# Down projection: tiles 15 to 18 as a second block group of seven products

## The chip, the cores and the metric

The kernel runs on one core of a Trainium2 chip. The metric is the device time of one execution in microseconds (us). TensorE (PE) multiplies; VectorE (DVE) and ScalarE (ACT) move results out of PSUM, the accumulators of PE, and prepare operands; GpSimd (POOL) and SyncE (SP) mostly issue DMA transfers here. Each engine works through its own queue in order, and waits at an instruction whose inputs or buffers aren't ready.

## The reference

A two-layer encoder over 1040 positions (16 learned ones and 1024 of the input) with 1024 channels. Each layer adds two things to the residual h: attention with its output projection, and a gated feed-forward network. The change lies in the last product of the second:

```
def conv_ffn(x, w_up, conv_w, conv_b, w_down):
    h = x @ w_up
    ...
    u, g = jnp.split(hc, 2, axis=-1)
    return (jax.nn.silu(g) * u) @ w_down

h = h + conv_ffn(rms_norm(h, ffn_norm[i]), w_up[i], conv_w[i], conv_b[i], w_down[i])
```

`w_down` has 2816 rows: 22 tiles of 128 channels. Everything is float32.

## The kernel before

**Numbers.** Channels lie on the 128 partitions, positions along the free axis. Each float32 operand of PE is split into a rounded part and the rest ("hi" and "lo", or ah and al), and a product is three matmuls: hi by hi, lo by hi, hi by lo (`mm3`, lines 254 to 256). Weights are loaded raw by SP, ACT casts the hi part, and DVE subtracts to get the lo part (lines 1132 and 1133 in `up_split`, 221 and 223 in `weights`).

**The down projection** sums 22 inner tiles for eight output tiles m of 128 channels and two halves of the positions (520 and 520 in layer 0, in pieces of 260 columns; 512 and 512 in layer 1, where the 16 learned positions are no longer wanted). It takes the inner tiles in five groups, listed in `GROUPS, LAST` (line 49):

- tiles 0 to 2, kind "n": for each m and half, all inner tiles are multiplied into one PSUM sum. ACT copies it to a buffer "do" (line 1677; three buffers in turn), and POOL adds that buffer to the residual tile `hm[m]` in DRAM with an accumulating DMA (line 1679).
- tiles 3 to 10, kind "s", a block group: two output tiles, the two halves of the positions and the two halves of the inner tiles make a 2 by 2 block product, done by Strassen's scheme (in Winograd's form) with seven products in place of eight. `down_blocks` has four pairs of output tiles, so 28 products, in an order written out by hand (`seq`). Each product needs a stationary operand made of the four raw weight blocks of its pair (A11, A12, A21, A22 and sums of them; `block_operand`, line 1114 for the sums), which is prepared `AHEAD` = 4 products ahead (`ensure`), and a moving operand X[p] made of the activations (`prepare`). The results are collected in two buffers of a pair, "du" and "dg" (ACT copies on line 1583, DVE adds on line 1582), and POOL adds them to `hm` in DRAM (lines 1600 and 1604). A buffer goes back to the pool of buffers `LANDING` = 4 products after its DMA was issued.
- tiles 11 to 14 and 15 to 18, kind "r": first SP loads the eight residual tiles from DRAM (`load_residual`, line 1650) into hT; then it goes as for "n", but DVE adds each PSUM sum to hT (line 1675).
- tiles 19 to 21 (`LAST`, in `down_last`): the same into hT, in three pieces of the positions; on the way the norm of what follows is fed (line 1754 the add to h, then the split for the next layer and the sum of squares, POOL's share of that on line 343), and hT is stored or, in layer 1, normalised and written out.

**What sets the order.** PE's order is that of the program text. For the other engines a scheduler orders instructions by its own estimate of when each is ready; it may put an instruction ahead of others that the text has before it. The activations were stored to DRAM by the up projection; `prepare` loads them ("st", line 1458), splits them for the plain groups (lines 1495 and 1496) or builds the fourteen buffers X[p] of a block group (lines 368, 369 and 1517). It is a generator that is advanced a step at a time by `pump`, called after each output tile of a plain group and at some products of a block group, where enough buffers are free. All these tiles share 33 buffers of one size, and six more (`ids`) that last through the feed-forward part of a layer; they are given out first in, first out. Raw weights have a ring of four buffers (tag "raw") and one of seven ("raw2"), operands two rings of three.

**Names that the change touches:** `GROUPS`, `LANDING`, `ensure` and `evacuate` and `run` in `down_blocks`, `load_residual`, `plain` and `run` in `ffn_down`.

Of the kernel before, what the change touches and what calls it, by code (L numbers as in the profile page):

```python
# [10 lines left out]
F32 = mybir.dt.float32  # L11
# [12 lines left out]
T = META + SEQ  # L24
KD = D // 128
# [20 lines left out]

GROUPS, LAST = (("n", 0, 3), ("s", 3, 8), ("r", 11, 4), ("r", 15, 4)), (19, 3)
HALVES, HALVES_LAST, HALVES_OUT = (0, 520, 520), (0, 520, 520), (16, 528, 512)  # L50
AHEAD = 4
LANDING = 4
FETCH = 60
SUB = 20
NSPLIT = 4
# [112 lines left out]
class Kern:  # L168
# [1383 lines left out]
            self.need = next(self.prep)  # L1552
            n -= 1

    def down_blocks(self, lyr, g0, ng, X, pp, fw, halves, after):
# [22 lines left out]
        going = []  # L1578

        def evacuate(i, j, p):  # L1580
            q = st[j]
            add = lambda out, ps: nc.vector.tensor_tensor(out=two(out), in0=ps[:, :pieces, :n], in1=two(out), op=ALU.add)
            copy = lambda out: nc.scalar.copy(two(out), q["a"][:, :pieces, :n])
            if p == 1:
                q["u"] = s.get(F32, "du")
                copy(q["u"][:, t0])
            elif p == 2:
                add(q["u"][:, t0], q["y"])
            elif p == 6:
                copy(q["u"][:, t1])  # L1590
            elif p == 7:
                q["g"] = s.get(F32, "dg")
                copy(q["g"][:, t1])
                if "x" in q:
                    add(q["g"][:, t1], q["x"])
            elif p == 5 and "g" in q:
                add(q["g"][:, t1], q["x"])
            elif p == 4:
                copy(q["g"][:, t0])
                nc.gpsimd.dma_start(self.hm[2 * j + 1][:, o0:T], q["g"][:, o0:T], accum_op=ALU.add)  # L1600
                going.append((i + LANDING, q["g"]))
            elif p == 3:
                add(q["u"][:, t1], q["x"])
                nc.gpsimd.dma_start(self.hm[2 * j][:, o0:T], q["u"][:, o0:T], accum_op=ALU.add)
                going.append((i + LANDING, q["u"]))
                del st[j]
        def run():
            self.among_blocks = True
            for i, (j, p) in enumerate(seq):
                ensure(i + AHEAD)  # L1610
                q = st.setdefault(j, {})
                bank, begins = {2: "y", 5: "x", 3: "x"}.get(p, "a"), p in (1, 2, 5)
                if begins:
                    place = {1: j % 2, 2: 3, 5: 2}[p]
                    q[bank] = pp.tile([128, 2, 512], F32, tag=f"p{place}", name="down", bufs=1)
                ps, w = q[bank], ops[i]
                ops[i] = None
                for k in range(nk):
                    _, hi, lo = X[p][k // 2]
                    for c in range(pieces):  # L1620
                        self.mm3(ps[:, c, :n], w[k], (hi[:, k % 2, :], lo[:, k % 2, :]), c * n, n,
                                 begins and k == 0, k == nk - 1, not begins)
                evacuate(i, j, p)
                while going and (going[0][0] <= i or i == len(seq) - 1):
                    s.put(going.pop(0)[1])
                if j == NP - 1:
                    for held, _, _ in X.pop(p):
                        s.put(*held)
                    if len(ops) == len(seq):
                        after()  # L1630
                    self.pump(1, 3)
                elif j and p == 5:
                    self.pump(1, 4)
            self.among_blocks = False
        return ensure, run

    def ffn_down(self, lyr, pp, fw, halves, acts, X, ids):
# [6 lines left out]
        two = lambda ap: ap.rearrange("p (a b) -> p a b", b=n)  # L1644
        hT, ahead, going = [], [], []

        def load_residual():
            for k in range(KD):
                hT.append(s.get(F32, f"h{k}", first=ids))
                nc.sync.dma_start(hT[k][:, o0:T], self.hm[k][:, o0:T])  # L1650

        def complete(done):
            while not done():
# [5 lines left out]
        def plain(kind, g0, ng, m, w, nxt):  # L1659
            if m == 0:  # L1660
                complete(lambda: all(j in acts for j in range(g0, g0 + ng)))
                if kind == "r" and not hT:
                    load_residual()
            if kind == "n" and m == 0:

                going.extend(s.get(F32, "do") for _ in range(3))
# [37 lines left out]
        def run():  # L1704
            blocks = None
            for i, part in enumerate(parts):
# [202 lines left out]
```

## Time and profile before

| | us |
|---|---|
| median of three runs | 2499.61 (2499.27 to 2500.78) |
| the profiled execution: its time | 2497.96 |
| the profiled execution: its span | 2496.2 |
| layer 0: tiles 11 to 14 and 15 to 18 on PE | 1122.1 to 1214.5 |
| layer 1: the same | 2357.9 to 2446.8 |

The time of an execution holds 1.8 us beside the span from the first to the last instruction. In the rows of stretches below, each engine has its busy time and, in brackets, its number of instructions; PEld is the weight load of PE, which runs beside the matmuls; PEclk is the granted clock of PE as a share of the full one; then come the mean busy share of the 16 DMA engines and what they moved. A row of a group has busy time and the mean of one in ns, and behind the second bar the idle time ahead of it with what ended it. In a row of waits stand the total, the number of times and the longest.

### The profile page before, as it was taken

The page shows a single profiled execution, that of the slowest core. Times are in us where ns is not written, and L with a number is a line of the kernel's source. Part 1 is how long each engine was busy: PE and PEld are TensorE (multiplying, and loading weights), DVE is VectorE, ACT ScalarE, POOL GpSimd, SP SyncE. Part 2 cuts the span into 40 slices and gives each one's busy share as a digit, 9 for nine tenths or more (in the row PEclk, how much of TensorE's full clock was granted, in tenths as well). Part 3 has the DMA queues.
Part 4 walks back from the last instruction along what each step waited for, and adds up shares of the span by engine and source line. Part 5 has one row for each costly group of instructions (what it writes and reads, how often), then busy time and mean ns, then how long its engine had stood idle before and what let it go on. Part 6 is the DMA issues. An engine that isn't in the chain of part 4 may idle for free.

```text
span 2496.2 us, 47323 instructions
## 1 busy us (share of the span) xinstructions
PE 2464.8 (99%) x18358; PEld 2370.8 (95%) x18358; DVE 1837.8 (74%) x3739; ACT 1298.1 (52%) x2811; POOL 385.4 (15%) x567
## 2 busy tenths in 40 slices
PE   9999999999999999999999999999999999999998
PEld 8989999999999999999999899999999999997886
DVE  8656776869988888854666666777699888887536
ACT  7346666636555555641343566665465555555412
POOL 2023333210000000100210334331100000001002
PEclk9999999999999999999999999999999999999999
DMA  3232134343322214763312222243423212247722
GB/s 134 68 88 72 43 97 129 124 126 103 112 84 73 90 65 148 194 172 118 106 56 73 75 78 73 67 147 105 147 88 104 90 66 94 92 151 179 197 72 81
DMA packets 118545, 261.02 MB, mean 105 GB/s; under 512 B 14880, under 2 KB 32544, under 8 KB 118320
## 3 DMA queue, kind: packets, MB, share of 16 engines
q1 hardware_dynamic: 93984, 182.81, 23.3%
q0 software_dynamic: 22464, 72.88, 10.4%
q8 instruction: 144, 2.36, 0.4%
q10 hardware_dynamic: 1872, 2.31, 0.3%
q14 instruction: 81, 0.66, 0.1%
HBM read 177.31 MB, written 67.85 MB: 98 GB/s over the span
## 4 chain that ended last, share of the span: by engine, by line
PE 67%; issue 16%; DVE 11%; ACT 5%; DMA 1%; POOL 0%; SPq 0%; DVEq 0%; POOLq 0%; ACTq 0%
PE mm L254 7%; PE mm L256 7%; PE mm L255 7%; PE up L254 5%; PE up L255 5%; PE up L256 5%; PE down L254 5%; PE down L255 5%; PE down L256 5%; PE av L752 3%; PE tr L726 2%; DVE S L693 1%; PE wo L254 1%; ACT P L705 1%; PE S L690 1%
## 5 line engine op out<-in xcount | busy, mean ns | idle before, releaser
L255 PE MATMUL up<-x,lo 128*128 128x260 f32 x2240 | 633.0, 283 | 0.0
L256 PE MATMUL up<-x,hi 128*128 128x260 f32 x2240 | 632.3, 282 | 0.3 <-DVE x L1157 0.3
L254 PE MATMUL up<-x,hi 128*128 128x260 f32 x2240 | 632.5, 282 | 0.0
L256 PEld LDWEIGHTS up<-x,hi 128*128 128x128 f32 x2240 | 422.2, 188 | 0.6 <-DVE x L1157 0.5
L254 PEld LDWEIGHTS up<-x,hi 128*128 128x128 f32 x2240 | 421.5, 188 | 0.4 <-DVE hg L1370 0.3
L255 PEld LDWEIGHTS up<-x,lo 128*128 128x128 f32 x2240 | 421.3, 188 | 0.1
L254 PE MATMUL mm<-xh,hi 128*128 128x348 f32 (+4 forms) x1056 | 362.6, 343 | 0.0
L256 PE MATMUL mm<-xl,hi 128*128 128x348 f32 (+4 forms) x1056 | 340.1, 322 | 0.0
L255 PE MATMUL mm<-xh,lo 128*128 128x348 f32 (+4 forms) x1056 | 339.5, 321 | 0.0
L1132 ACT CAST hi<-raw 128x512 fp32r<-128x512 f32 (+1 forms) x434 | 243.3, 572 | 150.7 <-PE up L256 88.2
L1133 DVE TENSOR_TENSOR lo<-raw,hi 128x512 fp32r<-128x512 f32 (+1 forms) x434 | 265.0, 624 | 76.0 <-ACT hi L1132 75.6
L254 PEld LDWEIGHTS mm<-xh,hi 128*128 128x128 f32 x1056 | 199.5, 189 | 5.2 <-issue 4.6
L255 PEld LDWEIGHTS mm<-xh,lo 128*128 128x128 f32 x1056 | 199.5, 189 | 0.7 <-issue 0.7
L256 PEld LDWEIGHTS mm<-xl,hi 128*128 128x128 f32 x1056 | 198.4, 188 | 0.4 <-issue 0.3
L221 ACT CAST hi<-raw 128x512 fp32r<-128x512 f32 (+2 forms) x168 | 97.3, 580 | 186.1 <-PE down L256 100.4
L254 PE MATMUL down<-ah,hi 128*128 128x260 f32 (+1 forms) x528 | 168.7, 320 | 0.5 <-ACT do L1677 0.5
L255 PE MATMUL down<-ah,lo 128*128 128x260 f32 (+1 forms) x528 | 168.5, 319 | 0.0
L256 PE MATMUL down<-al,hi 128*128 128x260 f32 (+1 forms) x528 | 168.3, 319 | 0.0
L705 ACT ACTIVATE P<-S,m 116x460 f32<-116x460 f32 (+2 forms) x224 | 124.8, 561 | 71.2 <-DVE m L693 67.5
L369 DVE TENSOR_TENSOR PT<-tr,PT 116x464 fp32r<-116x464 f32 (+3 forms) x240 | 122.9, 515 | 47.5 <-ACT PT L368 45.9
L1114 DVE TENSOR_TENSOR raw<-raw,raw 128x512 f32<-128x512 f32 x198 | 134.6, 686 | 24.1 <-DMA raw<-in_wd_dram 21.9
L1395 POOL DMA_DIRECT2D actd<-cv x44 | 23.6, 535 | 744.0 <-DVE cv L1394 725.9
(308 smaller groups left out, 5962.0 us busy)
## 6 DMA issues: line engine op xcount, KB each, us to landing
raw<-in_wm_dram SPq DMA_DIRECT2D x330, 256.0 KB, 2.9
raw<-in_wd_dram SPq DMA_DIRECT2D x64, 256.0 KB, 3.4
actd<-cv POOLq DMA_DIRECT2D x22, 520.0 KB, 3.0
actd<-cv POOLq DMA_DIRECT2D x22, 512.0 KB, 3.0
cb<-cd SPq DMA_DIRECT2D x16, 520.0 KB, 3.9
hm<-h POOLq DMA_DIRECT2D x32, 260.0 KB, 2.9
st<-actd SPq DMA_DIRECT2D x14, 520.0 KB, 4.4
st<-actd SPq DMA_DIRECT2D x14, 512.0 KB, 4.4
```

The source lines that it names most:

```text
L221: nc.scalar.copy(hi[:, :n, :], raw[:, :n, :])
L254: nc.tensor.matmul(ps, wh, xh[:, c0:c0 + n], start=first, stop=False, skip_group_check=more)
L255: nc.tensor.matmul(ps, wl, xh[:, c0:c0 + n], start=False, stop=False, skip_group_check=more)
L256: nc.tensor.matmul(ps, wh, xl[:, c0:c0 + n], start=False, stop=last, skip_group_check=more)
L369: nc.vector.tensor_tensor(out=lo, in0=src, in1=hi.bitcast(F32), op=ALU.subtract)
L690: nc.tensor.matmul(S[:rows, :n], q["qA"][e][:, qs], q["kA"][e][:, c0:k1], start=True, stop=False)
L705: nc.scalar.activation(P[:rows, :n], S[:rows, :n], AF.Exp, scale=-1.0, bias=m[:rows, nch - 1:nch], accum_out=(den if nch == 1 else d3[:row ...
L726: nc.tensor.transpose(tr[:w, 3 - j, :rows], P[:rows, o:o + w], id_)
L752: nc.tensor.matmul(av[:, a:b], w.rearrange("p a b -> p (a b)"), x, start=(t == ts[0] and part == 0 and i == 0), stop=(t == last and i == 1))
L1114: nc.vector.tensor_tensor(out=q[out][:, :nk, :], in0=q[a][:, :nk, :], in1=q[b][:, :nk, :], op=op)
L1132: nc.scalar.copy(hi[:, :nk, :], src[:, :nk, :])
L1133: nc.vector.tensor_tensor(out=lo[:, :nk, :], in0=src[:, :nk, :], in1=hi[:, :nk, :].bitcast(F32), op=ALU.subtract)
```

## The change

Tiles 11 to 14 become kind "n": ACT copies the sums to the three "do" buffers and POOL adds them to `hm` in DRAM. Tiles 15 to 18 become a second block group of 28 products with two inner tiles per side (nk = 2), half as long as those of the first. The residual stays in DRAM until that group: the tiles of a pair are loaded into hT by SP when both its buffers are given back (`summed`, the pairs 0 and 1), and the rest by POOL at the end of the group. In the second group a buffer is held for eight products instead of four, and the raw weights of the next pair are asked for at product 6 of a pair.

```diff
-GROUPS, LAST = (("n", 0, 3), ("s", 3, 8), ("r", 11, 4), ("r", 15, 4)), (19, 3)
+GROUPS, LAST = (("n", 0, 3), ("s", 3, 8), ("n", 11, 4), ("s", 15, 4)), (19, 3)
...
-LANDING = 4
+LANDING = {4: 4, 2: 8}
...
                 ops.append(self.block_operand(wd(2 * j), wd(2 * j + 1), nk, j, p, fw, raws, len(ops) % 2))
+                if nk == 2 and p == 6 and j + 1 < NP:
+                    self.block_raws(wd(2 * j + 2), wd(2 * j + 3), nk, j + 1, fw, raws)
...
-                going.append((i + LANDING, q["g"]))
+                going.append((i + landing, q["g"], 2 * j + 1))
...
                 while going and (going[0][0] <= i or i == len(seq) - 1):
-                    s.put(going.pop(0)[1])
+                    _, held, m = going.pop(0)
+                    s.put(held)
+                    landed.append(m)
+                    if len(landed) % 2 == 0 and i < len(seq) - 1:
+                        summed(landed[-2:])
...
-        def load_residual():
-            for k in range(KD):
-                hT.append(s.get(F32, f"h{k}", first=ids))
-                nc.sync.dma_start(hT[k][:, o0:T], self.hm[k][:, o0:T])
+        def load_residual(which, engine):
+            for k in sorted(which):
+                assert k == len(hT)
+                hT.append(s.get(F32, f"h{k}"))
+                engine.dma_start(hT[k][:, o0:T], self.hm[k][:, o0:T])
...
-                if kind == "r" and not hT:
-                    load_residual()
...
-                                              lambda t=then: len(ahead) < 2 and fetch(t))
+                                              lambda t=then: t and len(ahead) < 2 and fetch(t),
+                                              (lambda m: None) if then else lambda m: load_residual(m, nc.sync))
...
-            if not hT:
-                load_residual()
+            load_residual(range(len(hT), KD), nc.gpsimd)
```

More of the change, by code (lines that the diff above doesn't have):

```diff
@@ L1553, in pump, with down_blocks @@
             n -= 1
-    def down_blocks(self, lyr, g0, ng, X, pp, fw, halves, after):
+    def down_blocks(self, lyr, g0, ng, X, pp, fw, halves, after, summed):
         nc, s = self.nc, self.slots
@@ L1576, in ensure @@
                 ops.append(self.block_operand(wd(2 * j), wd(2 * j + 1), nk, j, p, fw, raws, len(ops) % 2))
-        going = []
+                if nk == 2 and p == 6 and j + 1 < NP:
+                    self.block_raws(wd(2 * j + 2), wd(2 * j + 3), nk, j + 1, fw, raws)
+        going, landed = [], []
+        landing = LANDING[nk]
         def evacuate(i, j, p):
@@ L1604, in evacuate @@
                 nc.gpsimd.dma_start(self.hm[2 * j][:, o0:T], q["u"][:, o0:T], accum_op=ALU.add)
-                going.append((i + LANDING, q["u"]))
+                going.append((i + landing, q["u"], 2 * j))
                 del st[j]
```

## The prediction

> **What bounds the kernel now.** I read the page's busy times first, then rows by stretch of the two down projections, then the waits of PE.
>
> ```profile
> PE 2464.8 (99%) x18358; PEld 2370.8 (95%) x18358; DVE 1837.8 (74%) x3739; ACT 1298.1 (52%) x2811; POOL 385.4 (15%) x567
> ...
> core 0: us, PE busy (x) PEld busy (x) DVE busy (x) ACT busy (x) POOL busy (x), PEclk, DMA share, GB/s
> 1007.00:1041.80 34.80, 34.80 (x294) 34.80 (x293) 33.73 (x37) 27.71 (x40) 6.56 (x8) 1.00 0.83 180
> 1041.80:1122.10 80.30, 80.30 (x673) 80.30 (x672) 40.59 (x56) 31.37 (x50) 5.94 (x7) 1.00 0.67 174
> 1122.10:1168.30 46.20, 46.20 (x389) 46.20 (x388) 20.52 (x29) 8.26 (x13) 1.70 (x2) 1.00 0.50 154
> 1168.30:1214.50 46.20, 46.20 (x387) 46.20 (x386) 16.36 (x25) 5.56 (x10) 0.00 (x0) 1.00 0.10 30
> 1214.50:1253.00 38.50, 37.56 (x233) 36.58 (x232) 31.25 (x56) 24.76 (x55) 19.37 (x20) 1.00 0.51 169
> ...
> 2280.50:2357.90 77.40, 77.40 (x334) 62.45 (x334) 40.26 (x58) 30.12 (x48) 5.96 (x7) 1.00 0.68 170
> 2402.30:2446.80 44.50, 44.50 (x195) 36.09 (x194) 16.06 (x24) 5.20 (x10) 0.00 (x0) 1.00 0.11 30
> 2446.80:2496.00 49.20, 37.76 (x232) 33.10 (x230) 33.98 (x70) 16.38 (x35) 14.47 (x14) 0.95 0.29 102
> ```
>
> The stretches of layer 0 are tiles 0 to 2, the first block group, tiles 11 to 14, tiles 15 to 18, and the last three tiles. PE is busy without a gap until 1214.5 us, at the full granted clock, and again from 2280.5 to 2446.8 in layer 1. So in these stages a matmul less is time less, as long as the other engines still keep up; DVE has 16.4 of 46.2 us of work in tiles 15 to 18, and the DMA engines are all but idle (0.10). Before, at the seam to the last three tiles, PE loses about 1 us to late weights:
>
> ```profile
> PE mm L254 <- ACT wl L221: 0.5, 1, 0.5
> PE mm L255 <- DVE wl L223: 0.5, 1, 0.5
> ...
> 1213.69 0.93 ACT L221 CAST wl<-raw 128x384 fp32r<-128x384 f32 x2 [15.81 <-PE down L255]
> ...
> 1213.56 2.37 DMA raw<-in_wd_dram
> ...
> PE down L254 <- ACT do L1677: 0.5, 1, 0.5
> ```
>
> The last of these rows is the one wait of PE in the down projection of layer 1 ahead of its end.
>
> **The change part by part.**
>
> *Matmuls removed.* Tiles 15 to 18 in layer 0 are 8 output tiles x 2 halves x 4 inner tiles x 2 pieces x 3 = 384 matmuls; as a block group they are 28 products x 2 inner tiles x 2 pieces x 3 = 336. The eighth of 46.2 us is 5.8, the eighth of 44.5 us in layer 1 is 5.6: together 11.4 us off the path, if nothing else gives way. The group then lasts 46.2 - 5.8 = 40.4 us, 1.44 us a product.
>
> *Tiles 11 to 14 as kind "n".* PE's part stays. DVE loses 16 adds, ACT gains 16 copies (below, 0.69 and 0.59 us), and POOL issues eight accumulating DMAs. Tiles 0 to 2 already run so, with the same eight DMAs in 34.8 us instead of 46.2, and with all of the larger first group's X built beside them (DVE 33.73 of 34.80 busy), without a gap on PE. I take 0.3 us for the one wait for a "do" buffer that layer 1 shows, and that has more room here.
>
> *X for tiles 15 to 18.* Seven casts on ACT and eleven operations of full width on DVE replace four casts and four subtractions:
>
> ```profile
> L1132 ACT CAST hi<-raw 128x256 fp32r<-128x256 f32 x98 | 38.5, 406 | 36.2 <-PE up L256 36.2
> L1133 DVE TENSOR_TENSOR lo<-raw,hi 128x256 fp32r<-128x256 f32 x98 | 39.5, 419 | 14.4 <-ACT hi L1132 14.2
> L1078 DVE TENSOR_TENSOR raw<-raw,raw 128x256 f32<-128x256 f32 x28 | 11.8, 420 | 0.5
> L369 DVE TENSOR_TENSOR x<-st,x 128x1040 fp32r<-128x1040 f32 x12 | 14.7, 1235 | 1.1 <-ACT x L368 1.1
> L1496 DVE TENSOR_TENSOR al<-st,ah 128x1040 fp32r<-128x1040 f32 x14 | 17.4, 1240 | 12.3 <-ACT ah L1495 12.3
> L1495 ACT CAST ah<-st 128x1040 fp32r<-128x1040 f32 x14 | 14.6, 1058 | 8.5 <-DMA st<-actd 8.5
> L1583 ACT COPY du<-down x16: 585/590/596, 1044.9 to 2339.2; 128x520 f32<-128x520 f32 x8, 128x512 f32<-128x512 f32 x8
> ...
> 1044.86 0.60 ACT L1583 COPY du<-down 128x520 f32<-128x520 f32 x1 [1.70 <-PE down L256]
> ...
> L1582 DVE TENSOR_TENSOR du<-down,du x16: 683/692/700, 1061.4 to 2361.6; 128x520 f32<-128x520 f32 x8, 128x512 f32<-128x512 f32 x8
> ```
>
> 11 x 1.24 = 13.6 us of DVE, spread by `pump` over 46.2 us of tiles 11 to 14, where DVE had 20.5 busy and loses 11: cost nothing, under PE.
>
> *The operands and sums of the second group.* Weight blocks are 256 wide. DVE: 28 lo parts x 0.42, 16 sums x 0.42, 12 adds x 0.69, and three of the last tiles' subtractions x 1.24: 11.8 + 6.7 + 8.3 + 3.7 = 30.5 of 40.4 us. ACT: 28 x 0.41, 16 x 0.59, 3 x 1.06 = 24.1 of 40.4 us. Both fit in the mean. What counts is each product's time: a copy out of PSUM must be done one product (1.44 us) later, when the next product goes on in the same sum. It takes 0.59 us and starts some 0.2 us after PE has moved on (the first group's first product ends at 1041.80 + 80.3 / 28 = 1044.67), which leaves 0.6; a cast of 1.06 us ahead of it takes that away. Bounds: nothing, since up-projection products with 256-wide blocks, beside which ACT did 98 such casts, run with PE full:
>
> ```profile
> 700.00:760.00 60.00, 60.00 (x504) 60.00 (x503) 51.83 (x82) 31.69 (x51) 1.59 (x3) 1.00 0.27 94
> ```
>
> and from above, what DVE waited for raw weights in the first group, where PE went on only because four products there are 11.5 us:
>
> ```profile
> DVE raw L1114 <- DMA raw<-in_wd_dram: 8.9, 1, 8.9
> ...
> DVE raw L1114 <- DMA raw<-in_wd_dram: 13.1, 2, 9.2
> ```
>
> The lead is now 4 x 1.44 = 5.8 us. A wait of 9.2 leaves 3.4 us uncovered, and two sums, a cast and a subtraction (4 x 0.42) have to follow: 5 us a layer at most for one such wait. It is nearer to nothing: those waits came while the DMA engines still had the sums of tiles 0 to 2 to land, and the raw weights of pairs 0 and 1 are now asked for during tiles 11 to 14; pair 2's are the first that the group itself asks for, some 10 us before PE needs them. I take 1.0 us a layer.
>
> *DMA.* The first group's own rows give the price of a byte:
>
> ```profile
> q1 hardware_dynamic: 3386, 9.31, 34.3%
> q0 software_dynamic: 1213, 4.45, 31.9%
> ...
> raw<-in_wd_dram SPq DMA_DIRECT2D x13, 256.0 KB, 5.1
> ...
> h<-hm SPq DMA_DIRECT2D x3, 520.0 KB, 4.8
> hm<-dg POOLq DMA_DIRECT2D x1, 520.0 KB, 8.6
> hm<-du POOLq DMA_DIRECT2D x1, 520.0 KB, 9.1
> ```
>
> Over 80 us, q0 needs 25.5 us for 4.45 MB (5.7 us a MB) and q1 27.4 for 9.31 (2.9). In the second group six sums (3.2 MB) cost 18 us, and 1.05 MB of raw weights, 1.6 of activations, 2.1 of residual and 0.8 of the next weights 16 us: 34 of 40.4, a share of 0.85 against 0.67 in the first group and 0.83 in tiles 0 to 2. Busy, not over. A half-sized raw block should land in 5 us or less. The Trainium skill's page "DMA: Bandwidth & Descriptors", section "Anatomy of one DMA", gives 2.0 us and the bytes over 436 GB/s for a transfer issued by GpSimd. That would be an estimated 3.2 us for one such sum; the rows say 8.6 and 9.1, and the measurement decides. By the page the two terms on late residual tiles below would be nothing, and the sum 11.4 - 3.3 = 8.1 us off.
>
> *The residual.* Tiles 0 to 3 come by SP inside the group, each behind its sum's landing. Tiles 4 to 7 come by POOL behind the end E. The sum of tile 6 is issued about 1.8 us after E (add 0.7, issue 0.85), lands 8 to 9 us later, and the load takes another 5: E + 15 to 16. The rows of before show when it is wanted:
>
> ```profile
> 1230.26 0.56 DVE L1754 TENSOR_TENSOR h<-mm,h 128x400 f32<-128x400 f32 x1
> ...
> 1222.46 3.76 POOL L343 TENSOR_TENSOR r<-r,sq 128x400 f32<-128x400 f32 x3 [95.87 <-ACT sq L342]
> ...
> 2461.77 0.69 DVE L1754 TENSOR_TENSOR h<-mm,h 128x512 f32<-128x512 f32 x1 [1.39 <-PE mm L256]
> ```
>
> Tile 7 in layer 0 at 1214.5 + 15.8, tile 6 in layer 1 at 2446.8 + 15.0. So DVE waits 1 us or so. POOL's sums of squares stand behind the two loads and start at E + 11 instead of E + 8, ACT behind them; eight PSUM banks let PE go on, and DVE has 7 us idle in the last three tiles of layer 0. Bounds: nothing, and 3 us in layer 1, whose end follows DVE. I take 0.5 us in all.
>
> *The seam.* The buffers of the last tiles' weights partly lie where the block group's operands lay, which are now in use up to E rather than 90 us earlier. Before, part of them waited for PE's end as well (the cast at 1213.69), for 1 us of PE. Bounds: 0 (as before) and 3 us a layer (a raw landing of 2.4 and a cast or two of 0.5); I take 0.5 more a layer, near what the rows of before show.
>
> *Sum.* -11.4 + 0.3 + 2 x 1.0 + 0.5 + 2 x 0.5 = -7.6 us. Against the profiled execution's 2497.96 us that is 2490.4; the median shown is 1.65 us above it, so for the median 2492.0.
>
> **The rivals.**
>
> *A. The residual holds SP: slower.* The scheduler places loads by its own estimate, and before it let SP stand in front of a residual tile whose sum had not landed:
>
> ```profile
> SPq L1650 <- DMA hm<-dg: 18.3, 2, 11.5
> ```
>
> Then nothing needed SP for 17 us. Now pair 3's raw weights and the activations 20 and 21 share the queue. If tile 0 (wanted from 12.5 us into the group, landed at 21 to 22.5) goes ahead of pair 3's blocks, these land at 27 or later, and product 18, due at 25.9, waits 3 us; with two holds (tiles 2 and 3 as well, at 31) and slow landings, 4 to 5 us each: 9 a layer. -11.4 + 18 - and 0.3 = +6.9, so 2506.5. It ends slower only from 8.2 us a layer on. For it: the hold of 11.5 us is shown, and the two sums' landings don't get faster. Against it: the loads stand in the text behind most of pair 3's blocks, whose buffers come free before.
>
> *B. The short lead eats the gain: no change.* One wait of DVE for raw weights of the size shown in each layer, and the dear end of the seam or the tail: 2 x 4 + 2 x 0.7 = 9.4 us against 11.4 - 0.3. That gives 2498.
>
> *C. All is hidden.* -11.4 + 0.3, a seam as before: 2488.5. For it stand the gapless rows of both the up projection and the first group.
>
> A rule that makes A and B dearer: where PE stands for long its granted clock falls. The trace has it at its end:
>
> ```profile
> 2484.00:2490.00 6.00, 2.11 (x10) 1.38 (x8) 5.96 (x17) 1.67 (x4) 0.00 (x0) 1.00 0.39 132
> 2490.00:2496.00 6.00, 0.00 (x0) 0.00 (x0) 3.11 (x8) 0.00 (x0) 0.00 (x0) 0.59 0.64 219
> ```
>
> With PE idle for four of six us the clock was still whole, and only beyond did it drop to a mean of 0.59; stalls of 1 us cost themselves alone. The Trainium skill, page "TensorE: Matmul & The Clock Gate", section "What's actually happening", has the clock halved after an idle window of about 3.4 us. By it a stall of 4 us in A would cost an estimated 1.7 us more, and A would end near 2512; the rows bear out no more than that long gaps do it.
>
> That the change doesn't do what it says (fewer matmuls, no shorter) is excluded by the full rows of PE, unless it waits.
>
> **How the numbers follow.** Forecast (2489.5 to 2494.6) 0.42, C 0.20, B 0.22, A 0.16. 0.2% of the median, about what a measurement here tells from no change, is 5.0 us. Forecast and C are faster by more: 0.62. B lies within 0.2%: 0.22. A is slower: 0.16. The predicted time is the forecast's, 2492.0. The range goes from 2487.5 (C, and the 1 us of the old seam gone too) to 2504 (B with some of A): outside lie A's larger part and little below. The forecast's own range is 2489 to 2495.
>
> **What would show it.** Right: the two groups of tiles 15 to 18 in about 40.4 and 38.9 us with PE busy for all but 1 us, DVE at 30 of 40, DMA share near 0.85, SP's longest hold before a residual tile ending before 22 us into the group; the start of the last three tiles with PE idle 1 to 2 us; tile 6's add to h at 15 us behind E. Wrong: waits of PE for "lo" of the second group above 3 us, a granted clock below 1.00 in it, DVE or ACT waiting for raw weights or activations over 6 us, PE waiting for weights of the last tiles over 3 us, or an idle PE in tiles 11 to 14 for a "do" buffer.

## The result, and the profile after

The changed kernel takes 2509.8 us (median, 2508.83 to 2512.05) beside 2500.0 us of the kernel before: a ratio of 1.0038, 95% interval 1.0026 to 1.005. It is slower by 9.8 us where 7.6 us less were forecast. Of its profiled execution (2512.05 us, span 2510.3) the page has the busy times:

```profile
PE 2463.2 (98%) x18286; PEld 2366.0 (94%) x18286; DVE 1846.5 (74%) x3785; ACT 1347.8 (54%) x2921; POOL 416.3 (17%) x607
```

PE issues 72 matmuls less, but its busy time is nearly the same (2464.8 before), and the span is longer by 14.1 us: PE stands, and part of its work runs at a lower clock. This execution is the slowest of its four, and that of before lies 2 us under its median, so these 14.1 us stand beside 9.8 in the medians. The rows by stretch of the changed kernel (columns as in the prediction) are the second block group and the last three tiles, first of layer 0, then of layer 1:

```profile
1168.40:1213.70 45.30, 42.21 (x339) 42.00 (x338) 23.92 (x48) 22.76 (x49) 6.48 (x8) 0.96 0.76 173
1213.70:1259.40 45.70, 38.97 (x234) 36.48 (x232) 30.14 (x55) 23.23 (x51) 22.11 (x24) 1.00 0.62 203
2414.80:2455.40 40.60, 39.41 (x171) 31.65 (x170) 23.75 (x48) 22.55 (x48) 6.10 (x8) 1.00 0.82 184
2455.40:2510.20 54.80, 39.67 (x231) 34.02 (x229) 33.14 (x70) 15.53 (x33) 18.06 (x20) 0.92 0.50 150
```

Measured between the starts of the same matmuls in both traces, layer 0's group went from 46.0 to 45.3 us (40.4 forecast), its last three tiles up to the next product from 37.8 to 45.7, that product from 30.0 to 32.5, layer 1's tiles 0 to 14 from 156.2 to 158.8, its group from 44.7 to 40.6, and the end from 49.2 to 54.9. Of the 2.6 us in layer 1's tiles 0 to 14, 1.6 fall in tiles 0 to 2; these take 33.3 to 35.9 us in the profiled executions of the kernels below, though no edit touches them, so this part is not shown to come from the change. The rest of the loss is in three places.

**In layer 0's group.** The waits of the changed kernel between 1168.4 and 1213.7 us (total, times, longest), SP's own last:

```profile
ACT wl L221 <- DMA raw<-in_wd_dram: 4.7, 1, 4.7
...
PE down L254 <- DVE du L1585: 3.1, 1, 3.1
...
SPq L1658 <- DMA hm<-dg: 10.2, 2, 7.6
SPq L1658 <- DMA hm<-du: 5.8, 2, 3.1
```

ACT's order of time in the same kernel shows what stood there:

```profile
1204.95 0.51 ACT L221 CAST wl<-raw 128x384 fp32r<-128x384 f32 x1 [4.69 <-DMA raw<-in_wd_dram]
1205.37 0.58 ACT L1586 COPY dg<-down 128x520 f32<-128x520 f32 x1
...
1206.26 0.41 ACT L1132 CAST hi<-raw 128x256 fp32r<-128x256 f32 x1
```

The scheduler had put a cast of the last tiles' weights into the group. Its raw weights came late, and behind it on ACT stood a PSUM copy and the cast of an operand of the group itself. DVE waited for that cast, with the PSUM adds behind it for which PE waited:

```profile
1206.70 0.42 DVE L1133 TENSOR_TENSOR lo<-raw,hi 128x256 fp32r<-128x256 f32 x1 [5.07 <-ACT hi L1132]
1207.04 1.30 DVE L1585 TENSOR_TENSOR du<-down,du 128x520 f32<-128x520 f32 x2
```

The raw weights were late because SP asked for them late. Its rows (neighbours are joined) have two residual loads, the second behind a sum that took until then to land, and right behind it this load, which landed 3.6 us later:

```profile
1197.41 3.83 SPq L1658 DMA_DIRECT2D h<-hm  x2
1201.35 14.95 SPq L212 DMA_DIRECT2D raw<-in_wd_dram  x6
```

PE's rows by stretch around it:

```profile
1200.00:1204.70 4.70, 4.70 (x40) 4.49 (x38) 1.64 (x5) 0.26 (x1) 0.00 (x0) 1.00 0.67 227
1204.70:1208.00 3.30, 0.21 (x2) 0.21 (x2) 1.30 (x3) 2.21 (x5) 0.85 (x1) 1.00 0.51 98
1208.00:1213.70 5.70, 5.70 (x36) 5.70 (x36) 1.04 (x2) 1.20 (x3) 1.40 (x2) 0.70 0.97 199
```

After 3.1 us without work the granted clock was 0.70 on the mean of 5.7 us (0.50 in the first 3.4 of them), which is another 0.30 x 5.7 = 1.7 us. The Trainium skill, page "TensorE: Matmul & The Clock Gate", section "What's actually happening", has the clock halved after an idle window of about 3.4 us; the trace agrees nearly, with 3.1 us.

**In layer 0's last three tiles.** From DVE's order of time, the changed kernel:

```profile
1214.90 1.03 DVE L223 TENSOR_TENSOR wl<-raw,wl 128x384 fp32r<-128x384 f32 x2 [3.47 <-DMA hm<-du]
...
1221.26 0.56 DVE L223 TENSOR_TENSOR wl<-raw,wl 128x384 fp32r<-128x384 f32 x1 [1.56 <-ACT wl L221]
1221.74 0.57 DVE L1760 TENSOR_TENSOR h<-mm,h 128x400 f32<-128x400 f32 x1
...
1223.56 0.57 DVE L1760 TENSOR_TENSOR h<-mm,h 128x400 f32<-128x400 f32 x1
1226.64 0.42 DVE L237 TENSOR_TENSOR both<-raw,both 128x256 fp32r<-128x256 f32 x1 [2.52 <-ACT both L236]
...
1229.34 1.05 DVE L1760 TENSOR_TENSOR h<-mm,h 128x400 f32<-128x400 f32 x2
```

The first add to h comes 8.0 us after the stage's first matmul (before: 1217.4 against 1214.3, 3.1 us), since the subtractions for the last weights stand ahead of it. Between the second and the third add lie 5.8 us (before: 0.9), in which ACT and DVE wait for the weights of the next product ("both"); their loads of 256 KB landed after 8.2 us, 3.7 before (medians of 1195 to 1235 us). No add of this stage waited for a residual tile. What follows has no room, as the changed kernel's waits between 1207 and 1264 us show:

```profile
ACT xh L329 <- DVE h L1760: 12.7, 14, 1.5
...
DVE xl L330 <- ACT xh L329: 7.0, 19, 0.7
...
PE mm L254 <- ACT wl L221: 4.8, 1, 4.8
```

The add on DVE, the cast on ACT and the rest on DVE wait for one another, for eight tiles in three pieces; a late start of this chain is a late end. From the fourth of its 24 adds to the last it takes 31.4 us before and 31.3 in the changed kernel, and the fourth comes 8.2 and 16.1 us behind the stage's first matmul. The last row is the next product's wait for its own weights, whose cast stands behind the chain on ACT. After these 4.8 us the granted clock was 0.50 for 6.8 us (before, it was whole there), and that product took 2.5 us more.

**At the end of layer 1.** DVE's and POOL's order of time in the changed kernel:

```profile
2459.28 1.03 DVE L223 TENSOR_TENSOR wl<-raw,wl 128x384 fp32r<-128x384 f32 x2 [5.64 <-issue]
2460.22 0.68 DVE L1585 TENSOR_TENSOR du<-down,du 128x512 f32<-128x512 f32 x1
...
2475.03 2.62 DVE L1760 TENSOR_TENSOR h<-mm,h 128x512 f32<-128x512 f32 x6 [5.11 <-DMA h<-hm]
```

```profile
2461.21 0.88 POOL L1607 DMA_DIRECT2D hm<-du  x1 [0.24 <-DVE du L1585]
...
2471.49 11.76 POOL L343 TENSOR_TENSOR r<-r,sq 128x512 f32<-128x512 f32 x10
```

Tile 6 reached DVE 19.6 us behind the group's end E (2455.4). Its sum was issued at E + 5.8: the last add to it on DVE stood behind subtractions for the last weights, which waited 5.6 us. The profile names nothing for that wait; the same subtractions in layer 0 waited for hm<-du. POOL's sums of squares, behind the last two residual loads, ended at 2483.3.

### The profile page after: what moved, and what is told of

The parts are those of the page before. It is cut to its first block, busy times and chain, and to the rows that moved or that the text cites. A ratio compares the mean times of both kernels' runs of the same rounds, so it can differ in the third digit from the quotient of the medians.

```text
span 2510.3 us, 47481 instructions
## 1 busy us (share of the span) xinstructions
PE 2463.2 (98%) x18286; PEld 2366.0 (94%) x18286; DVE 1846.5 (74%) x3785; ACT 1347.8 (54%) x2921; POOL 416.3 (17%) x607
## 4 chain that ended last, share of the span: by engine, by line
PE 62%; issue 17%; DVE 12%; ACT 5%; DMA 3%; POOL 1%; SPq 0%; DVEq 0%; POOLq 0%; ACTq 0%
PE mm L254 7%; PE mm L255 6%; PE mm L256 6%; PE up L254 5%; PE up L255 5%; PE up L256 5%; PE down L255 5%; PE down L256 5%; PE down L254 5%; PE av L752 3%; PE tr L726 2%; DVE S L693 1%; PE S L690 1%; ACT P L705 1%; PE S L691 1%
## 5 line engine op out<-in xcount | busy, mean ns | idle before, releaser
L1133 DVE TENSOR_TENSOR lo<-raw,hi 128x512 fp32r<-128x512 f32 (+1 forms) x490 | 288.6, 603 | 119.8 <-ACT hi L1132 119.3
L1132 ACT CAST hi<-raw 128x512 fp32r<-128x512 f32 (+1 forms) x490 | 265.6, 553 | 169.9 <-PE up L256 88.2
L1114 DVE TENSOR_TENSOR raw<-raw,raw 128x512 f32<-128x512 f32 (+1 forms) x230 | 148.0, 651 | 48.3 <-DMA raw<-in_wd_dram 45.8
L254 PE MATMUL down<-x,hi 128*128 128x260 f32 (+1 forms) x504 | 162.1, 322 | 4.3 <-DVE du L1585 3.1
L255 PE MATMUL down<-x,lo 128*128 128x260 f32 (+1 forms) x504 | 161.9, 321 | 0.4 <-DVE lo L1133 0.4
L256 PE MATMUL down<-x,hi 128*128 128x260 f32 (+1 forms) x504 | 161.7, 321 | 0.0
L1371 ACT COPY hg<-up 128x520 f32<-128x520 f32 x88 | 52.2, 593 | 151.2 <-PE up L256 151.2
```

The costliest lines, as they stand in the source:

```text
L254: nc.tensor.matmul(ps, wh, xh[:, c0:c0 + n], start=first, stop=False, skip_group_check=more)
L255: nc.tensor.matmul(ps, wl, xh[:, c0:c0 + n], start=False, stop=False, skip_group_check=more)
L256: nc.tensor.matmul(ps, wh, xl[:, c0:c0 + n], start=False, stop=last, skip_group_check=more)
L1114: nc.vector.tensor_tensor(out=q[out][:, :nk, :], in0=q[a][:, :nk, :], in1=q[b][:, :nk, :], op=op)
L1132: nc.scalar.copy(hi[:, :nk, :], src[:, :nk, :])
L1133: nc.vector.tensor_tensor(out=lo[:, :nk, :], in0=src[:, :nk, :], in1=hi[:, :nk, :].bitcast(F32), op=ALU.subtract)
```

## The experiments

Each time is a median beside runs of the kernel before on the same chip (2499.9 to 2501.3 us). Stages in us, between the starts of PE's matmuls in each profiled execution (the start of a group is read up to 0.3 us early, in all rows alike). The profiled execution is the slowest one of the changed kernel, and the fastest one with the sums on POOL and with the casts behind.

| kernel | group, layer 0 | last three | group, layer 1 | end | median | ratio (95%) |
|---|---|---|---|---|---|---|
| before | 46.0 | 37.8 | 44.7 | 49.2 | 2500.0 | |
| changed | 45.3 | 45.7 | 40.6 | 54.9 | 2509.8 | 1.0038 (1.0026 to 1.005) |
| e1, no landing | 48.2 | 43.8 | 44.9 | 48.9 | 2509.6 | 1.0038 (1.0023 to 1.0053) |
| e2, all late | 40.4 | 48.1 | 39.2 | 54.9 | 2509.3 | 1.0039 (1.0024 to 1.0053) |
| e6, sums on POOL | 42.8 | 42.3 | 41.2 | 49.0 | 2500.7 | 0.9999 (0.9989 to 1.0008) |
| e6, sums on DVE | 40.4 | 39.3 | 39.2 | 49.4 | 2491.6 | 0.9965 (0.9953 to 0.9976) |
| e8, early residual | 40.4 | 43.4 | 39.2 | 49.0 | 2497.5 | 0.9984 (0.9975 to 0.9994) |
| e8, hold only | 40.5 | 43.2 | 39.2 | 49.0 | 2497.1 | 0.9987 (0.9977 to 0.9996) |
| e10, own buffers | 44.0 | 46.5 | 41.1 | 53.3 | 2510.6 | 1.0042 (1.0027 to 1.0057) |
| e7, sums only | – | 37.1 | – | 49.0 | 2498.6 | 0.9992 (0.9983 to 1.0002) |
| e11, first four late | 40.4 | 44.3 | 39.2 | 51.7 | 2505.9 | 1.002 (1.001 to 1.0031) |
| e12, last four late | 40.4 | 46.0 | 39.2 | 55.1 | 2512.2 | 1.0048 (1.0033 to 1.0063) |
| e9, small sums | 40.4 | 41.2 | 39.1 | 48.9 | 2492.1 | 0.9965 (0.9954 to 0.9977) |
| e5, casts behind | 40.4 | 46.3 | 39.1 | 52.6 | 2509.5 | 1.0036 (1.0024 to 1.0049) |
| e13, plain writes | 40.5 | 43.2 | 39.1 | 49.1 | 2497.8 | 0.9991 (0.9981 to 1.0) |
| e4, loads last | 42.7 | 44.8 | 39.8 | 52.8 | 2504.9 | 1.0016 (1.0006 to 1.0027) |

(The dashes: no second group. Tiles 0 to 18 take 207.0 us in layer 0 and 200.0 in layer 1 there, 206.9 and 200.9 in the kernel before.)

**Is it the wait for the sums?**

```diff
-                engine.dma_start(hT[k][:, o0:T], self.hm[k][:, o0:T])
+                engine.dma_start(hT[k][:, o0:T], self.hT0[k, :, o0:T])
```

> The changed kernel, but the residual tiles are loaded from the kernel's input, which nothing writes, instead of from the running sum in DRAM: same number and size of loads on the same engines, nothing to wait for. It leaves out the true values of the residual (the attention's and the groups' sums aren't in it), no work. Theory 1, the round trip: the changed kernel loses because SP stands behind sums that haven't landed (10.2, 7.6, 5.8 and 3.1 us in layer 0's second group, with the last tiles' raw weights queued behind) and because tiles 4 to 7 come late. Then the layer 0 group falls from 45.2 to about 41 us, layer 0's last three tiles lose their late start, and the time is 2489 to 2495 us. Rival, the short products: ACT and DVE with a lead of two 128x256 blocks are what is late. Then the group stays at 44 to 45 us and the time stays above 2503 us.

Theory 1 missed, and the rival's time came for another reason than its own. The late end of layer 1 is gone (48.9), so there the wait for the landing was the cause. But both groups got longer: without a wait the loads start early, and collide with the weights: the group's own raw blocks of 128 KB landed after 6.6 us, and after 2.1 in the changed kernel (medians of 1168 to 1214 us). The rows by stretch and a wait of this kernel's group in layer 0:

```profile
1169.50:1217.70 48.20, 44.02 (x339) 43.60 (x338) 23.43 (x48) 22.76 (x49) 8.24 (x12) 0.93 0.76 184
```

```profile
DVE raw L1114 <- DMA raw<-in_wd_dram: 11.2, 2, 6.3
```

DVE waits there for raw weights, it isn't short of time. The same traffic came to the same time here, lost elsewhere.

**Loads taken out of the group.**

```diff
-  (lambda m: None) if then else lambda m: load_residual(m, nc.sync))
+  lambda m: None)
```

> The changed kernel, but no residual tile is loaded inside the second block group: all eight are loaded behind it on POOL. It undoes the part that makes SP stand for the sums inside the group, and makes the lateness of the residual larger. Theory 1: the raw weights of the last three tiles are no longer behind SP's wait, so the 3.1 us idle of PE in layer 0's second group and the low clock after it go and the group takes 40.5 to 42 us instead of 45.2; but the first add of the last three tiles then waits for tile 0, and the stage behind grows by 5 to 12 us a layer: 2513 to 2530 us in all. Rival, the short products: the group stays at 44 to 45 us, and the stage behind grows as well.

The group is what was forecast for it, and the last three tiles pay; the time came out below the expected range. Its rows by stretch:

```profile
1167.70:1208.10 40.40, 40.40 (x339) 40.40 (x339) 24.00 (x48) 22.66 (x48) 8.26 (x11) 1.00 0.79 183
1208.10:1256.20 48.10, 39.49 (x235) 36.47 (x233) 30.18 (x55) 23.55 (x51) 22.68 (x25) 1.00 0.65 201
```

PE is full at a DMA share of 0.79: the short products themselves cost nothing.

**Residual in SBUF, sums added there.**

```diff
-("n", 11, 4), ("s", 15, 4)
+("r", 11, 4), ("s", 15, 4)     # residual loaded at tile 11, as before
...
-                nc.gpsimd.dma_start(self.hm[2 * j][:, o0:T], q["u"][:, o0:T], accum_op=ALU.add)
+                nc.vector.tensor_tensor(out=h, in0=t[:, o0:T], in1=h, op=ALU.add)   # or nc.gpsimd
```

> Tiles 15 to 18 as a second group of seven products, as in the changed kernel, but the residual stays in SBUF: it is loaded at the start of tiles 11 to 14 as before the change, those tiles add to it there (as before), and the eight sums of the second group are added to it by POOL instead of by DMA. Theory 1, the round trip costs what is lost: without it the 11.4 us of matmuls removed come through less 1 to 3 us, 2488 to 2492 us; POOL has eight sums of about 2.6 us (two of its 1304 ns for 128x512), 21 of 40 us. Rival, the short products: the layer 0 group still takes 44 us or more and the time is 2498 us or more.

> The same with the eight sums on DVE instead of POOL. DVE has eight operations of about 1.24 us more (its rate for 128x1040), 10 us, in a group of 40 us in which it has about 10 us left. Theory 1: 2489 to 2497 us, 1 to 5 us over the version with POOL, and PE waits for operands (lo) in the group. Rival, the short products: those waits come to 5 us a layer or more and the time is 2500 us or more.

With DVE the change pays: 0.9965, which beats the kernel before by 8.8 us and the changed kernel by some 18. The expected order of the two was wrong: POOL was to be the faster, at 2488 to 2492 us, and with DVE PE was to wait for operands, of which its full rows show nothing. The rows by stretch with DVE:

```profile
1169.50:1209.90 40.40, 40.40 (x339) 40.40 (x338) 31.26 (x56) 22.31 (x48) 0.00 (x0) 1.00 0.16 46
1209.90:1249.20 39.30, 37.28 (x234) 36.57 (x232) 32.36 (x56) 22.77 (x50) 19.33 (x19) 1.00 0.46 153
2402.40:2441.60 39.20, 39.20 (x171) 31.73 (x170) 31.02 (x56) 22.20 (x48) 0.00 (x0) 1.00 0.17 48
```

The groups of costliest instructions in layer 0's group say why POOL is dearer; first with POOL's sums, then with DVE's:

```profile
L1133 DVE TENSOR_TENSOR lo<-raw,hi 128x256 fp32r<-128x256 f32 x23 | 17.0, 755 | 3.7 <-ACT hi L1132 3.7
...
L1592 DVE TENSOR_TENSOR du<-down,du 128x520 f32<-128x520 f32 x7 | 4.7, 685 | 0.0
```

```profile
L1133 DVE TENSOR_TENSOR lo<-raw,hi 128x256 fp32r<-128x256 f32 x23 | 9.1, 416 | 2.4 <-ACT hi L1132 2.3
...
L1592 DVE TENSOR_TENSOR du<-down,du 128x520 f32<-128x520 f32 x7 | 4.8, 690 | 0.0
```

**The sums back as DMAs, without and with SP's waits.** In the first, the residual is loaded at tile 11 and the sums go to DRAM as in the change; the second adds this where the change has SP load a tile:

```diff
+                nc.sync.dma_start(self.look[k][:, lyr, :], self.hm[k][:, o0:o0 + 16])
```

> The residual is loaded at the start of tiles 11 to 14 and these tiles add to it in SBUF, as before the change; the second group's eight sums still go to DRAM by the same accumulating DMAs, and nobody reads them (so they are left out of the output). Beside the version with the sums on DVE it puts the eight DMAs back, beside the changed kernel it takes away the residual loads in and behind the group. Theory H, SP's hold: it was the loads of the residual behind unlanded sums that cost; then layer 0's second group takes 40 to 41 us, its last three tiles up to the next product 38 to 39.5 us (before: 37.8), and the time is 2489 to 2494 us. Theory S, the seam: the last tiles' weights get buffers that the sums' DMAs are still reading (3.5 us, DVE wl behind DMA hm<-du, in the changed kernel); then the group is short but the stage behind it takes 42 us or more, and the time is 2496 us or more.

> The same, but where the changed kernel loads a residual tile on SP (tiles 0 to 3 in the second group), SP issues a copy of 16 of its columns from the running sum to a scratch place in DRAM: the same wait for the same sums at the same places in SP's queue, with 8 KB instead of 520 KB to move. Theory H, the hold: layer 0's second group takes 44 us or more again, with PE waiting for operands or copies in it, and the time is 3 to 6 us over the version without these waits. Theory C, crowded DMA engines: without the traffic the waits cost nothing, the group takes 40 to 41 us and the time is within 1.5 us of the version without them.

The eight DMAs alone cost 6 us beside the sums on DVE, 4.1 of it in layer 0's last three tiles. The DMA rows of 1168 to 1214 us, first with these DMAs, then with DVE's sums (median us to landing):

```profile
q0 software_dynamic: 974, 3.65, 44.8%
...
raw<-in_wd_dram SPq DMA_DIRECT2D x8, 192.0 KB, 5.0
```

```profile
raw<-in_wd_dram SPq DMA_DIRECT2D x8, 192.0 KB, 2.4
```

The last tiles' raw weights land in 5.0 instead of 2.4 us (3.6 in the changed kernel). The stage and the time are those of theory S. SP's waits in the version with the hold, 1169 to 1264 us:

```profile
SPq L1663 <- DMA hm<-dg: 7.8, 2, 4.5
SPq L1663 <- DMA hm<-du: 5.2, 2, 2.8
```

SP stood 13.0 us (16.0 in the changed kernel), and nothing came of it: 2497.1 against 2497.5 us. So the hold by itself, without the residual's bytes, is free, and theory H fell. In the changed kernel it is a link all the same. SP issued the late load there 32.8 us into the group, and here 30.6: the second pair's sums, for which SP stands, landed after 7.5 and 9.6 us there, and after 5.4 and 7.2 here. How long ACT's cast then waited for that load, and PE in the group, goes together in five kernels of the table: 4.7 and 3.1 us in the changed one, 3.6 and 2.0 in e4, 3.4 and 1.8 in e10, 1.5 and nothing in this one, 0.7 and nothing in e2. ACT can wait 1.6 us there before PE does.

**The buffers at the seam.** The changed kernel again, but the buffers under way go back only behind the last weights' allocation:

```diff
-                    s.put(held)
+                    if nk == 2 and i == len(seq) - 1:
+                        self.under_way.append(held)      # put back in down_last
+                    else:
+                        s.put(held)
```

> The changed kernel, but the buffers of the sums that are still under way when the second group's products end go back only after the last three tiles' weights have got theirs, so no such weight waits for a sum to leave its buffer. Theory S: DVE's wait for hm<-du (3.5 us) at the end of layer 0's second group goes, the first add of the last three tiles comes 3 to 4 us earlier, the stage falls from 45.7 to 41 or 43 us, and the time is 2503 to 2507 us. Theory H, or the raw weights themselves late: the stage stays at 45 us or more and the time within 1.5 us of 2509.5 us.

DVE's wait for hm<-du is gone from the list, but the time is unchanged and theory S missed: the next late thing took its place. The first add of the last three tiles comes 2.7 us behind the stage's first matmul, but the fourth 18.6 (16.1 in the changed kernel), as ACT waits 6.1 us in all for the next product's weights.

**Tiles 11 to 14 alone.**

```diff
-("n", 11, 4), ("s", 15, 4)
+("n", 11, 4), ("r", 15, 4)     # residual loaded at tile 15
```

> Tiles 11 to 14 alone changed (their products copied by ACT and summed to DRAM), tiles 15 to 18 plain as before with the residual loaded at their start: no second block group, no matmul removed. It prices the part that the prediction costed at 0.3 us. By that step: 2500 to 2502 us. If the eight sums more and the later residual cost of themselves (first adds of tiles 15 to 18 waiting for tile 0's sum and load): 2503 to 2508 us.

It costs nothing (1.4 us under the expected range, with an interval that holds no change).

**Halves of the residual.**

```diff
+            if kind == "x":
+                kind = "r" if m in early else "n"      # early = range(4, 8), then range(0, 4)
```

> Residual tiles 4 to 7 are loaded at the start of tiles 11 to 14 and added to in SBUF; tiles 0 to 3 go as in the changed kernel (ACT copies, sums in DRAM, reloaded by SP inside the second block group). The second group's sums for tiles 4 to 7 stay in DRAM and are left out of the output. It is half of what lies between the version with all eight tiles early (2497.5 us) and the changed kernel (2509.8 us). Theory P, each half has its own price: the four loads in the group crowd out weights there; layer 0's second group takes 43.5 to 46 us, the end of layer 1 (from the last three tiles' first product) stays at 49 us, and the time is 2501 to 2506 us. Rival, only all eight together crowd: the group takes 40 to 41 us and the time is 2496 to 2499 us.

> The other half: tiles 0 to 3 early and in SBUF (their sums of the second group are left out of the output), tiles 4 to 7 as in the changed kernel, reloaded by POOL behind the group. Theory P: the groups take 40 to 41 and 39 to 40 us, but the end of layer 1 takes 53 to 55 us instead of 49, layer 0's last three tiles 44 to 46 us, and the time is 2502 to 2507 us. Rival, the late tiles are late only because the group's own loads hold up the sums: the end takes 49 to 50 us and the time is 2496 to 2500 us.

They don't divide the loss cleanly: mixing the kinds cost both 5.4 to 5.9 us of its own in tiles 0 to 14 of layer 0 (160.8 us in the changed kernel, 166.2 and 166.7 here). So 2505.9 lies in theory P's range by luck, with a group that isn't the one it forecast, and 2512.2 lies above it. Behind that, both groups are full in both, so it takes more than either half to make the group stall; tiles 4 to 7 late make the end 55.1 us, tiles 0 to 3 51.7 us.

**The traffic of the sums.**

```diff
+        few = T - o0 if nk == 4 else 64
...
-                nc.gpsimd.dma_start(self.hm[2 * j][:, o0:T], q["u"][:, o0:T], accum_op=ALU.add)
+                nc.gpsimd.dma_start(self.hm[2 * j][:, o0:o0 + few], q["u"][:, o0:o0 + few], accum_op=ALU.add)
```

> The changed kernel, but each of the second group's eight sums adds 64 columns to DRAM instead of 1040 or 1024 (the rest of these sums is left out of the output). Waits, buffers, the residual's loads and their places stay; the sums' traffic goes and each lands sooner. Theory T, traffic: the sums and the loads share the DMA engines, and the sums' long landing is what makes the loads late; then the layer 0 group takes 40 to 41.5 us, its last three tiles 38.5 to 41 us, the end 49 to 51 us, and the time is 2491 to 2497 us. Rival L, the loads cost where they stand: the group takes 43 us or more or the end 53 us or more, and the time is 2501 to 2506 us.

Theory T: 17.7 us less than the changed kernel, with every wait, buffer and residual load in its place. SP's holds in front of the residual tiles shrink as well, from 16.0 to 7.3 us in all, since the sums land sooner; this run doesn't part the two. Rows by stretch:

```profile
1168.00:1208.40 40.40, 40.40 (x339) 40.40 (x338) 25.04 (x50) 22.88 (x49) 7.90 (x10) 1.00 0.62 157
1208.40:1249.60 41.20, 37.26 (x235) 36.55 (x233) 29.42 (x53) 23.23 (x51) 21.24 (x22) 1.00 0.49 164
...
2442.30:2491.10 48.80, 37.53 (x231) 32.92 (x229) 32.92 (x68) 15.10 (x33) 16.50 (x17) 0.94 0.32 109
```

**ACT's order.** The last weights of the changed kernel behind the group's last copy on ACT:

```diff
+            with self.tc.issue_after(self.last_copy.ins):
                 w.append(self.weights(self.wd[lyr, m][:, g0:g0 + ng, :], ...
```

> The changed kernel, but the casts of the last three tiles' weights stand behind the second group's last PSUM copy on ACT (in the changed kernel two stand inside the group, and one of them waits 4.7 us there for its raw weights, with PSUM copies behind it). Theory Q, ACT's order: PE's 3.1 us idle in layer 0's second group and the low clock after it go, the group takes 41 to 42.5 us instead of 45.3, and what is won is partly lost behind it, where the last weights now come later: 2505 to 2509 us. Rival: the second group's own raw weights are late as well, the group stays at 44 us or more, and the time at 2509 us or more.

In the profiled execution (2502.3 us) the stall is gone and the group takes 40.4 us, so the cast was the link to PE. But the executions lie between 2502.3 and 2511.5 us, and their median is that of the changed kernel: on the time the run is inconclusive, and what most executions lose, no trace here shows.

**Adding, or bytes?**

```diff
-  ..., q["u"][:, o0:T], accum_op=ALU.add)
+  ..., q["u"][:, o0:T])        # second group only
```

> The changed kernel, but the second group's eight sums are plain writes of the same 1040 or 1024 columns (they overwrite the running sum in DRAM instead of adding to it, so what was there is left out of the output). Queue, bytes written, buffers, waits and the residual's loads stay; only the adding goes. Theory A, the adding: it is what makes a sum land after 7 to 9 us and hold the DMA engines; then most of what the small sums won (17.7 us) is won here too: layer 0's group 40 to 41.5 us, its last three tiles 39 to 42.5 us, the end 49 to 51 us, the time 2492 to 2499 us. Rival B, the bytes written: 2505 to 2510 us.

Theory A, at two thirds of its size: 12.0 us less, the groups and the end as short as with small sums, the last three tiles not (43.2). DMA rows of 1168 to 1214 us, first of the changed kernel, then with plain writes:

```profile
hm<-dg POOLq DMA_DIRECT2D x3, 520.0 KB, 6.1
hm<-du POOLq DMA_DIRECT2D x3, 520.0 KB, 7.7
```

```profile
q0 software_dynamic: 1448, 5.33, 35.1%
...
hm<-dg POOLq DMA_DIRECT2D x4, 520.0 KB, 4.2
hm<-du POOLq DMA_DIRECT2D x4, 520.0 KB, 4.5
```

On that queue a MB now takes 0.351 x 46 / 5.33 = 3.0 us of all 16 engines (loads among it), beside 0.448 x 46 / 3.65 = 5.6 us where it holds sums alone.

**POOL's order.**

```diff
+            with self.tc.issue_after(self.last_sum.ins):
+                load_residual(range(len(hT), KD), nc.gpsimd)
```

> The changed kernel, but on POOL the loads of residual tiles 4 to 7 stand behind the last pair's two sums, where two of them stood in front (and held these sums up to 3.5 us). Theory O, POOL's order: tiles 6 and 7 come 3 to 5 us earlier, the end of layer 1 takes 50 to 53 us instead of 54.9, and the time is 2504 to 2508 us. Rival, the DMA engines set it: the sums and loads take what they took, the end stays at 54 us or more and the time at 2509 to 2511 us.

By its time theory O: 4.9 us less than the changed kernel. By its mechanism only in part: tile 7's sum was issued 4.9 us sooner behind the group's end, but tile 6's, which waits for its add on DVE, 7.8 us behind it (5.8 in the changed kernel), and its add to h came at 18.5 instead of 19.6 us. The end is 2.1 us shorter. Layer 0's group is shorter by 2.6 us too, and it lies ahead of the loads that were moved; so how much of the 4.9 us is POOL's order is not shown.

## Why the prediction was wrong

The cause, in medians:

| the second group's sums | residual reloaded in and behind the group | residual in SBUF from tile 11 on |
|---|---|---|
| added in DRAM by DMA | 2509.8 | 2497.5 |
| plain writes | 2497.8 | |
| 64 columns | 2492.1 | |
| added in SBUF by DVE | | 2491.6 |

The sums alone cost 5.9 us, the reload with hardly any sums next to nothing (2492.1), both together some 18. Together they land late (the second pair's sums after 7.5 and 9.6 us, and after 5.4 and 7.2 without the reload's bytes), and three short deadlines stand right behind: the weights of the last tiles and of the next product, residual tiles 4 to 7, and the group's own operands queued behind a cast. In the profiled execution 14.1 us were lost where 7.6 were to be won. Of these 21.7 us, against the terms of the forecast, 7.4 lie in layer 0's last three tiles, 4.7 at layer 1's end, 3.9 in layer 0's group and 2.5 in the product behind its last tiles.

*Matmuls removed: right.* Where nothing stalls, the groups take 40.4 and 39.1 to 39.2 us (40.4 and 38.9 forecast).

*Tiles 11 to 14, X: right.* No measurable cost in layer 0, where PE's time for tiles 0 to 14 is 160.8 us, before 1168.3 - 1007.4 = 160.9; with tiles 11 to 14 alone changed the time didn't rise.

*Operands and sums of the second group, 1.0 us a layer: too much by itself.* Nothing in nine versions with a full group; DVE was less busy than worked out (24.0 of 40.4 us with all loads late, 30.5 forecast). In the changed kernel PE did stand: not for the group's own raw weights, but for PSUM adds behind an operand whose cast stood behind one that belongs to the stage after; that hoisted cast was not in the working. With the clock it cost 4.8 us in layer 0.

*DMA: the price was right, what followed from it wrong.* 5.7 and 2.9 us a MB were forecast, and the changed kernel's rows of 1168 to 1214 us give 0.485 x 46 / 3.94 = 5.7 and 0.275 x 46 / 3.97 = 3.2, and shares of 0.76 and 0.82 where 0.85 stood:

```profile
q0 software_dynamic: 1064, 3.94, 48.5%
q1 hardware_dynamic: 2160, 3.97, 27.5%
```

"Busy, not over" is a mean: what counted was when single loads of the next weights were asked for and landed. The price by the Trainium skill's page "DMA: Bandwidth & Descriptors", section "Anatomy of one DMA" (an estimated 3.2 us for a sum) fits neither the sums (6.1 and 7.7 us) nor the plain writes (4.2 and 4.5).

*The residual, 0.5 us in all: failed in layer 1.* Tile 6 came at 19.6 us behind E, not 15 to 16. Its sum was to be issued 1.8 us behind E and was issued at 5.8, as its add on DVE stood behind late weights; layer 1's end lost 5.7 us where the upper bound was 3. In layer 0 no add waited for a residual tile. But there "DVE has 7 us idle" was counted as room. That idle time is the chain's own waiting (31.4 and 31.3 us from the fourth add on), and it gives nothing back.

*The seam, 0.5 us a layer: the step that was furthest off.* Layer 0's last three tiles lost 7.9 us with the residual reloaded beside them, and 5.6 us with the residual in place but the sums as DMAs (43.4 against 37.8). The bound of 3 us came from a single landing of 2.4. It left out that a weight's buffer would wait for a sum (3.5 us), that the next product's weights would land in 8.2 us, and that the chain behind passes every delay on.

*Rival A* had the sign and, with 2506.5, nearly the size. Its mechanism, SP's hold, is a link in layer 0's group, on the last tiles' weights and not on pair 3's, and it costs nothing without the residual's bytes; the larger losses lie behind the groups, so that the size came out is luck. *The clock* was right as a rule for long gaps, and here 3.1 us were long enough. The range went up to 2504, for one stall in each group, 0.7 us a layer behind it and some of rival A; behind the groups layer 0 lost 7.9 and 2.5 us, and layer 1 5.7.

Open stays where the slower executions of the version with the casts behind lose their time, and how the 1.5 us that the best version still loses in layer 0's last three tiles would come back; PE waits 2.1 us there for the next product's weights (0.5 before).

## What to carry to other kernels

Where a stage's traffic grows, don't stop at the mean DMA share: list the few loads that the next stage starts with, and ask what each landing costs if it doubles, because here the work put on idle DMA engines was paid at the seam. Adding in DRAM cost about twice the DMA time of a write here (5.6 against 3.0 us a MB); with 16 of 40 us free on DVE, adding in SBUF was cheaper and took the landing out of every later wait. Idle time between two engines that wait for each other is no slack: whatever starts such a chain late ends it late.

## What the runs showed of the hardware

DVE's subtraction of two SBUF operands took 755 instead of 416 ns on the mean while POOL was adding in SBUF (15.7 us of 42.8), and its add with one operand in PSUM stayed at 685 and 690 ns. This had not been expected. The version with POOL is 9 us slower than that with DVE, and its groups are 2.4 and 2.0 us longer; that all 9 us come from this is not shown. The Trainium skill, page "SBUF — State Buffer", section "Who interferes with whom", says that a DVE instruction with two SBUF inputs contends with a GpSimd instruction that reads SBUF, and one with at most one such input does not: the trace agrees on both.
